# Scores' products with the keys' low parts: 64 rows each, in pairs in the two halves of the array, and attention in pieces of 256 queries

## The chip, the cores and the metric

The kernel runs on one core of one Trainium2 chip. The metric is the device time of one execution in microseconds (us), as a median of several runs. The kernel before takes 960.17 us (three runs, 958.83 to 961.95).

The core has a matrix engine (TensorE, PE in the profile; its weight loads are listed as PEld), VectorE (DVE), ScalarE (ACT), GpSimd (POOL) and SyncE (SP), which issues nearly all DMAs. Matrix products land in PSUM, which has eight buffers of 128 partitions by 512 floats (banks).

## The reference

One layer of an encoder block over 512 positions of width 2048, in float32: adaptive RMSNorm, one projection, two token mixers side by side, a gated output projection and a final RMSNorm. The change touches the first mixer, attention with 16 heads of 64:

```python
aq, ak, av, ag, gq, gk, gv, gg, lr_f, lr_b = jnp.split(h @ w_in[layer], PROJ_SPLITS, axis=-1)
for window, dilation in ((128, 1), (512, 4), (2048, 16)):
    o_p, lse_p = dilated_window_attention(aq, ak, av, rel_bias, window, dilation)
    ...
mix_w = jax.nn.softmax(jnp.stack(lses, axis=0), axis=0)
att = jnp.einsum('pbsh,pbshe->bshe', mix_w, jnp.stack(outs, axis=0))
```

Inside, logits are `q.k / 8` plus a bias by distance, with a mask. Three window softmaxes merged by their denominators are one softmax over all 512 keys, in which a key counts as often as it lies in a window: the kernel computes that, with the logarithm of this multiplicity in the bias.

## The kernel before

**Precision.** TensorE multiplies a rounded float32 format (`F32R`, fp32r in the profile). To keep float32 accuracy the kernel splits operands into a rounded high part and the rest, the low part, and sums the products high x high, low x high and high x low (`three`, lines 168 to 171: three matmuls, each with its own weight load). A matmul has a stationary operand (the weights, up to 128 rows by 128 columns) and a moving one (the same rows by up to 512 columns).

**Stages.** First a starting stage computes the normalised input and a first part of the projection (`sta`, `stb` in the profile). Then the projection goes on in units of 512 columns (`unit`, line 843): `qk2`, `qk4`, `qk6` (queries and keys of two pairs of heads each), `gk`, then `gv0` and so on for the second mixer, and the output projection. A unit has four tiles of 128 columns (in PSUM buffers with the tag `pj`, five of them) and eight groups of weights, each fetched on SP one or two groups ahead, and split into high and low part by ScalarE (L313) and VectorE (L297). One call of `three` is a tick; a unit has 64.

**Side work.** Into a unit's stream of matmuls, work of other kinds is hung at given shares of its ticks. TensorE's order is the order of the program. Side items are emitted with a raised priority; the order on the other engines is set by a scheduler from priorities and dependences, ahead of time, so that on the chip each engine works off a fixed queue. A side item due at share `at` is emitted after the first tick that is at least 64 x `at`; an item due at 1 or later goes over into the next unit. The sums for the gates (`rawv`, `rawg`) are other side work, on VectorE.

**Attention** (`attention`, line 556) is side work of the units `qk2`, `qk4`, `qk6` and `gk`, four heads in each call. It works in tiles of 128 queries: 16 tiles in a call, and for each

- `score` (line 567): two matmuls (L576, L577) into a PSUM buffer with the tag `pa`, of which there are three; VectorE adds the bias and finds the row minimum (L580), ScalarE takes the exponential (L583), VectorE the reciprocal (L584), GpSimd scales (L585). The result is `p`.
- `turn` (line 589), two tiles later: four transposes (L597) of `p` into a `pa` buffer, which ScalarE (L601) and VectorE (L602) evict as high and low part, `pt`.
- `values` (line 605), once for two tiles, a half: eight matmuls (L611) of `pt` with the values, into a `pa` buffer, evicted by ScalarE (L614) and VectorE (L618).

The items of a call are spread evenly over 0.8 of the unit's ticks from 0.17 on (`ATT_AT`), the first two moved forward by 0.04 and 0.05, the last moved back by 0.05, into the next unit.

**Operands of the scores.** `qk_evict` (line 531) runs after the unit that made a pair of heads. Each head has 64 rows in the banks `psq` and `psk`. For a head, `qs` has 128 rows: the high part of the queries (ScalarE, L539) in the head's own half of the rows, the low part (VectorE, L540) in the other half. `ks` has the keys' high part in both halves, `kl` the keys' low part in both: own half by an engine (L548, L550), the other by a DMA. So

```python
mm(ps, qs[:, q], ks, start=True, stop=False)   # high x high + low x high
mm(ps, qs[:, q], kl, start=False, stop=True)   # high x low  + low x low
```

The banks of the first two pairs come from the starting stage: its eight tiles use the five `pj` buffers and the three `pa` buffers, in which stand the keys of the first pair and queries and keys of the second.

Of the kernel before, what the change touches and what calls it, by code (L numbers as in the profile page):

```python
# [10 lines left out]
F32 = mybir.dt.float32  # L11
F32R = mybir.dt.float32r
I32 = mybir.dt.int32
AF = mybir.ActivationFunctionType
ALU = mybir.AluOpType
# [3 lines left out]
P = 128  # L19
# [114 lines left out]
def block_kernel(ctx: ExitStack, tc: tile.TileContext, a: dict):  # L134
    nc = tc.nc
# [6 lines left out]
    sm = ctx.enter_context(tc.tile_pool(name="sm", bufs=4))  # L142
# [4 lines left out]
    def T2(name, dt=F32, parts=P):  # L147
        return t2.tile([parts, 512], dt, tag="t2", name=name)

    def B8(name, shape, dt=F32):  # L150
        return b8.tile([P] + shape, dt, tag="b8", name=name)
# [4 lines left out]
    def PA(name):  # L156
        return pp.tile([P, 512], F32, tag="pa", bufs=3, name=name)

    mm = nc.tensor.matmul
    tt = nc.vector.tensor_tensor  # L160
    stt = nc.vector.scalar_tensor_tensor
    act = nc.scalar.activation
# [69 lines left out]
    for j in range(4):  # L232
        ch, cl = c_parts[2 * j][64:65, :], c_parts[2 * j + 1][64:65, :]
        src = first[64:65, 512 * j:512 * j + 512]
# [92 lines left out]
    scale = cst.tile([P, KT], F32, tag="scale", name="scale")  # L327
# [149 lines left out]
    n = len(chain) // 2  # L477
    for z in range(2):
        task(("row", z), "DVE", 0.66, [("ul", 0)], 950, lambda z=z: bias_row_out(z), None, "b8" if z else None)
    for i in range(n):  # L480
        mm_task(i)
        st, k, j = chain[i]
# [15 lines left out]
    for i in range(n, 2 * n):  # L498
        mm_task(i)
        st, k, j = chain[i]  # L500
# [3 lines left out]
    for w in range(4):  # L504
        for kt in range(4):
            j, g = w // 2 * 4 + kt, w % 2
# [22 lines left out]
    stacks = {}  # L529

    def qk_evict(p, psq, psk):

        for j in range(2):
            own = slice(64 * j, 64 * j + 64)
            oth = slice(64 - 64 * j, 128 - 64 * j)
            qs = T2(f"qs{p}{j}", F32R)
            act(qs[own], psq[own, ::-1], AF.Copy, scale=-0.125)  # L539
            stt(qs[oth], psq[own, ::-1], -0.125, qs[own].bitcast(F32),  # L540
                op0=ALU.mult, op1=ALU.subtract)
            stacks[2 * p + j] = [qs, None, None, own]
        for j in range(2):
            own = slice(64 * j, 64 * j + 64)
            oth = slice(64 - 64 * j, 128 - 64 * j)
            ks = T2(f"ks{p}{j}", F32R)
            kl = T2(f"kl{p}{j}", F32R)
            act(ks[own], psk[own], AF.Copy)  # L548
            nc.sync.dma_start(ks[oth].bitcast(F32), ks[own].bitcast(F32))
            tt(kl[own], psk[own], ks[own].bitcast(F32), op=ALU.subtract)  # L550
            nc.sync.dma_start(kl[oth].bitcast(F32), kl[own].bitcast(F32))
            stacks[2 * p + j][1:3] = ks, kl
# [2 lines left out]

    def attention(pairs):

        tiles = [(2 * p + j, i) for p in pairs for j in range(2) for i in range(4)]
        gt, pt, pr_ = {}, {}, {}
        heads = [2 * p + j for p in pairs for j in range(2)]  # L560

        def g_load(h):
            g = gp.tile([P, 896], F32, tag="g", name=f"g{h}")
            nc.sync.dma_start(g, bass.AP(grow.tensor, grow.offset + h * 1024, [[1, P], [1, 896]]))
            gt[h] = g

        def score(h, i):
            def go():
                if h % 8 == 0 and i == 0:
                    cat[h // 8] = B8(f"cat{h // 8}", [4, 512])  # L570
                if i == 1 and h != heads[-1]:
                    g_load(h + 1)
                qs, ks, kl, _ = stacks[h]
                q = slice(P * i, P * i + P)
                ps = PA(f"s{h}{i}")
                mm(ps, qs[:, q], ks, start=True, stop=False)  # L576
                mm(ps, qs[:, q], kl, start=False, stop=True)  # L577
                t = T2(f"p{h}{i}")
                st = sm.tile([P, 3], F32, tag="st", name=f"st{h}{i}", bufs=6)
                nc.vector.tensor_tensor_reduce(  # L580
                    out=t, in0=ps, in1=gt[h][:, P * i:P * i + 512], op0=ALU.add, op1=ALU.min,
                    scale=1.0, scalar=3e38, accum_out=st[:, 0:1])
                act(t, t, AF.Exp, bias=st[:, 0:1], scale=-1.0, accum_out=st[:, 1:2])  # L583
                nc.vector.reciprocal(st[:, 2:3], st[:, 1:2])  # L584
                nc.gpsimd.tensor_scalar(t, t, st[:, 2:3], 1.0, op0=ALU.mult, op1=ALU.mult)  # L585
                pr_[h, i] = t
            return go

        def turn(h, i):
            def go():  # L590
                half, ii = divmod(i, 2)
                if ii == 0:
                    pt[h, half] = B8(f"pt{h}{half}", [2, 4, 256], F32R)
                t = pr_.pop((h, i))
                pk = PA(f"t{h}{i}")
                for kt in range(4):
                    nc.tensor.transpose(pk[:, kt * P:kt * P + P], t[:, kt * P:kt * P + P], ident)  # L597
                hi = pt[h, half][:, 0, :, P * ii:P * ii + P]
                lo = pt[h, half][:, 1, :, P * ii:P * ii + P]
                src = pk.rearrange("p (k q) -> p k q", k=4)  # L600
                act(hi, src, AF.Copy)  # L601
                tt(lo, src, hi.bitcast(F32), op=ALU.subtract)  # L602
            return go

        def values(h, half):
            def go():
                t = pt.pop((h, half))
                po = PA(f"o{h}{half}")
                for kt in range(4):
                    for w in range(2):  # L610
                        mm(po[:, :256], vv[h // 4][:, kt, h % 4, :], t[:, w, kt, :],  # L611
                           start=kt == 0 and w == 0, stop=kt == 3 and w == 1)
                oh = sm.tile([64, 256], F32, tag="oh", name=f"oh{h}{half}", bufs=1)
                act(oh, po[64:128, :256], AF.Copy)  # L614
                own = stacks[h][3]
                p = h // 2
                dst = cat[p // 4][own, p % 4, 256 - 256 * half:512 - 256 * half]
                tt(dst[:, ::-1], po[0:64, :256], oh, op=ALU.add)  # L618
            return go

        items = []
        n = len(tiles)
        for x in range(n + 4):
            if x < n:
                items.append(score(*tiles[x]))
            if 2 <= x <= n + 1:
                items.append(turn(*tiles[x - 2]))
            if 3 <= x <= n + 2 and tiles[x - 3][1] % 2 == 1:
                items.append(values(tiles[x - 3][0], tiles[x - 3][1] // 2))
        g_load(heads[0])  # L630
        start, span, move0, move1, move_last = ATT_AT
        at = [start + (q + 0.5) / len(items) * span for q in range(len(items))]
        at[0] -= move0
        at[1] -= move1
        at[-1] += move_last
        return list(zip(at, items))
# [52 lines left out]
    def some_sums(name):  # L689
        r = [sum_work.pop(0) for _ in range(SUMS_IN.get(name, len(sum_work)))]  # L690
        n = len(r)
        loads = [(max(q - 0.3, 0.1) / n, x[0]) for q, x in enumerate(r)]
        return sorted(loads + [((q + 0.7) / n, x[1]) for q, x in enumerate(r)], key=lambda x: x[0])
# [206 lines left out]
    for p in range(2):  # L900
        qk_evict(p, psb["b", 4 + 2 * p], psb["b", 5 + 2 * p])
    for n, p in (("qk2", 0), ("qk4", 2), ("qk6", 4)):
        ps = unit(n, False, attention((p, p + 1)) + ([(0.05, shift_row)] + some_sums(n) if p == 4 else []))
        for q in range(2):
            qk_evict(p + 2 + q, ps[2 * q], ps[2 * q + 1])

    ps = unit("gk", False, attention((6, 7)) + some_sums("gk"))
    gla["k"] = B8("gkt", [4, 512])
    for i in range(4):
# [17 lines left out]
    ps = unit("gv0", True, some_sums("gv0"), lr=lr_tick)  # L927
# [20 lines left out]
    ps = unit("gv1", True, gla_head(0) + some_sums("gv1"))  # L948
# [3 lines left out]
    for j in range(2):  # L952
        ps = unit(f"ag{j}", False, gla_head(1 + j) + some_sums(f"ag{j}"))
        gate_evict(ps, cat[j], f"a{j}", vbias[:, 4 * j:4 * j + 4])
    ps = unit("gg0", False, gla_head(3) + some_sums("gg0"))
# [16 lines left out]
    ps = unit("gg1", False, side + some_sums("gg1"))  # L972
# [43 lines left out]
    for j in range(3):  # L1016
# [3 lines left out]
        ps = unit(f"o{j}", True, side, rhs=rhs)  # L1020
# [22 lines left out]
    for tiles in ((0, 1), (2,), (3,)):  # L1043
        ps = unit("o3", True, rhs=rhs, tiles=tiles)
# [86 lines left out]
```

## Time and profile before

| | |
|---|---|
| median of three runs | 960.17 us (958.83 to 961.95) |
| the profiled execution | 959.9 us, of which the instructions span 957.9 us |
| TensorE busy / weight loads | 98% / 81% of the span |
| VectorE, ScalarE, GpSimd busy | 63%, 45%, 8% |
| granted TensorE clock, mean | 0.997 |
| attention's matmuls | from 198.0 to 459.1 us |
| of these: scores | 64 with `ks`, 64 with `kl`, each 128 rows by 512 columns |

Times inside an execution are counted from the span's start. A row of a timeline has start, duration, engine, line, operation, the tiles (out <- in, buffer numbers left out), sizes and count; in brackets stands the idle time of the engine before it, and what ended it. Matmuls are pipelined: a record's duration is longer than the distance to the next, and its end is modelled.

### The profile page before, as it was taken

Reading aid. Unit: us, or ns where it says so; the run is one execution under the profiler, and the core shown is the slowest. Engines: PE = TensorE matmul, PEld = TensorE weight load, DVE = VectorE, ACT = ScalarE, POOL = GpSimd, SP = SyncE. Lnnn points to the kernel's source line nnn. Section 1 sums busy time; section 2 is a strip of 40 time slices with the busy share of each in tenths; the row PEclk is TensorE's granted clock in tenths of the full one; section 3 lists DMA queues with packets and bytes.
Section 4 is the critical chain, followed back from the end, with each engine's and each line's share of the span. In section 5 each row is a group of like instructions: output and inputs, shape, how many; then the busy total and the mean of one; then the engine's idle time right before and its main releaser. Section 6 shows DMA issues by size and latency. Waiting matters only on the chain.

```text
span 957.9 us, 11999 instructions
## 1 busy us (share of the span) xinstructions
PE 939.7 (98%) x4464; PEld 777.1 (81%) x4464; DVE 605.3 (63%) x900; ACT 431.5 (45%) x719; POOL 81.1 (8%) x100
## 2 busy tenths in 40 slices
PE   8999999999999999999999999999999999999996
PEld 5888788888888888888778888888887888888884
DVE  7988899675756676766435656675964352546421
ACT  5443533565655655655215544543834152233222
POOL 0000000012122022122000000000010000202120
PEclk9999999999999999999999999999999999999998
DMA  9999687443333463533454244354555464244013
GB/s 330 413 411 365 229 296 275 150 131 105 112 103 105 144 200 108 173 127 103 150 176 146 86 132 154 132 176 154 173 195 183 132 221 154 92 151 152 23 55 121
DMA packets 45180, 163.76 MB, mean 171 GB/s; under 512 B 5730, under 2 KB 6018, under 8 KB 40386
## 3 DMA queue, kind: packets, MB, share of 16 engines
q1 hardware_dynamic: 44946, 162.68, 49.9%
q8 instruction: 35, 0.57, 0.2%
q10 hardware_dynamic: 176, 0.33, 0.1%
q14 instruction: 23, 0.18, 0.1%
HBM read 154.51 MB, written 4.28 MB: 166 GB/s over the span
## 4 chain that ended last, share of the span: by engine, by line
PE 84%; DMA 6%; DVE 5%; issue 3%; ACT 1%; SPq 0%; POOL 0%; ACTq 0%; DVEq 0%; POOLq 0%
PE ps_o L170 6%; PE ps_o L169 6%; PE ps_o L171 6%; DMA rawg<-in_wg 6%; PE ps_qk L170 5%; PE ps_qk L169 5%; PE ps_qk L171 5%; PE o L611 3%; PE sta L169 3%; PE sta L170 3%; PE sta L171 3%; PE stb L171 3%; PE stb L169 3%; PE stb L170 3%; PE ps_gv L171 3%; PE ps_gv L170 3%
## 5 line engine op out<-in xcount | busy, mean ns | idle before, releaser
L585 POOL TENSOR_SCALAR p<-p,st 128x512 f32<-128x512 f32 x64 | 45.5, 711 | 406.6 <-DVE st L584 357.9
L244 DVE CUSTOM_DVE_ANT_0 cb<-cb,sb,c_bcond 128x2048 f32<-128x2048 f32 (+1 forms) x32 | 73.4, 2294 | 0.0
L583 ACT ACTIVATE p<-p,st 128x512 f32<-128x512 f32 x64 | 46.1, 721 | 56.8 <-DVE st L580 56.3
L602 DVE TENSOR_TENSOR pt<-t,pt 128x512 fp32r<-128x512 f32 x64 | 44.0, 689 | 16.2 <-ACT pt L601 15.8
L580 DVE CUSTOM_DVE_ANT_0 p<-s,g 128x512 f32<-128x512 f32 x64 | 43.6, 687 | 14.8 <-PE s L577 14.5
L601 ACT ACTIVATE pt<-t 128x512 fp32r<-128x512 f32 x64 | 37.8, 592 | 10.2 <-PE t L597 9.2
L244 DVE CUSTOM_DVE_ANT_0 rawg<-rawg,sb,gate 128x1024 f32<-128x1024 f32 x16 | 20.5, 1283 | 29.6 <-DMA rawg<-in_wg 29.6
L611 PEld LDWEIGHTS o<-pt,vv 128*128 128x128 f32 x256 | 34.7, 188 | 5.0 <-DVE pt L602 2.2
L597 PEld LDWEIGHTS t<-c_ident,p 128*128 128x128 f32 x256 | 31.8, 140 | 8.5
L597 PE MATMUL t<-c_ident,p 128*128 128x128 f32 x256 | 38.3, 272 | 0.0
L611 PE MATMUL o<-pt,vv 128*128 128x256 f32 x256 | 36.6, 283 | 0.9 <-DVE pt L602 0.8
L244 DVE CUSTOM_DVE_ANT_0 rawg<-rawg,sb,c_bcond 128x1024 f32<-128x1024 f32 x16 | 20.5, 1283 | 26.3 <-DMA rawg<-in_wg 26.3
L1014 POOL TENSOR_TENSOR x<-x,fgain 128x512 f32<-128x512 f32 x12 | 20.3, 1696 | 185.3 <-ACT ysq L1012 185.3
L1012 ACT ACTIVATE ysq<-x 128x512 f32<-128x512 f32 x16 | 10.1, 632 | 47.2 <-DVE x L1010 47.2
L767 POOL TENSOR_SCALAR dc<-st,sc 128x256 f32<-128x256 f32 x16 | 10.4, 652 | 245.5 <-DVE st L764 240.6
L1009 DVE TENSOR_TENSOR y<-ps_o,sb 128x512 f32<-128x512 f32 x16 | 10.9, 684 | 25.9 <-PE ps_o L171 25.9
L584 DVE RECIPROCAL st<-st 128x1 f32<-128x1 f32 x64 | 10.3, 162 | 24.9 <-ACT p L583 24.9
L576 PE MATMUL s<-ks,qs 128*128 128x512 f32 x64 | 25.1, 391 | 0.0
L577 PE MATMUL s<-kl,qs 128*128 128x512 f32 x64 | 25.0, 391 | 0.0
L774 ACT ACTIVATE sq<-st,sc 128x256 f32<-128x256 f32 x24 | 12.2, 509 | 26.8 <-DVE st L769 14.3
L1010 DVE TENSOR_TENSOR x<-y,x 128x512 f32<-128x512 f32 x16 | 18.0, 1125 | 0.3
L614 ACT ACTIVATE oh<-o 64x256 f32<-64x256 f32 x32 | 12.2, 382 | 13.0 <-PE o L611 12.2
(1275 smaller groups left out, 2916.7 us busy)
## 6 DMA issues: line engine op xcount, KB each, us to landing
cb<-in_wm SPq DMA_DIRECT2D x31, 1024.0 KB, 7.9
rawg<-in_wg SPq DMA_DIRECT2D x32, 512.0 KB, 3.4
raw_o<-in_w_o SPq DMA_DIRECT2D x32, 512.0 KB, 3.4
raw_qk<-in_w_qk SPq DMA_DIRECT2D x24, 512.0 KB, 3.4
rawb<-in_w_sb SPq DMA_DIRECT2D x16, 512.0 KB, 4.8
rawv<-in_wv SPq DMA_DIRECT2D x16, 512.0 KB, 3.8
raw_gv<-in_w_gv SPq DMA_DIRECT2D x16, 512.0 KB, 3.5
raw_ag<-in_w_ag SPq DMA_DIRECT2D x16, 512.0 KB, 3.3
```

What stands on the lines that cost most here:

```text
L169: mm(ps, lh, rh, start=first, stop=False)
L170: mm(ps, ll, rh, start=False, stop=False)
L171: mm(ps, lh, rl, start=False, stop=last)
L244: nc.vector.tensor_tensor_reduce(out=w, in0=w, in1=with_, op0=ALU.mult, op1=ALU.add, scale=1.0, scalar=init, accum_out=dst)
L576: mm(ps, qs[:, q], ks, start=True, stop=False)
L580: nc.vector.tensor_tensor_reduce(out=t, in0=ps, in1=gt[h][:, P * i:P * i + 512], op0=ALU.add, op1=ALU.min, scale=1.0, scalar=3e38, accum_o ...
L583: act(t, t, AF.Exp, bias=st[:, 0:1], scale=-1.0, accum_out=st[:, 1:2])
L585: nc.gpsimd.tensor_scalar(t, t, st[:, 2:3], 1.0, op0=ALU.mult, op1=ALU.mult)
L597: nc.tensor.transpose(pk[:, kt * P:kt * P + P], t[:, kt * P:kt * P + P], ident)
L601: act(hi, src, AF.Copy)
L602: tt(lo, src, hi.bitcast(F32), op=ALU.subtract)
L611: mm(po[:, :256], vv[h // 4][:, kt, h % 4, :], t[:, w, kt, :], start=kt == 0 and w == 0, stop=kt == 3 and w == 1)
```

## The change

- `qk_evict`: in the blocks 0 and 2 of 128 queries the high part stays in the head's own rows and the low part in the others; in the blocks 1 and 3 the two change places. Each of the two instructions per head becomes two, over 2 x 128 columns each.
- `score` takes a half (two blocks, 256 queries) and two `pa` buffers. Both products with `ks` come first, over 128 rows as before. The product with `kl` takes only the rows with the queries' high part: own rows for the first block, the other rows for the second. The two stand in different halves of the array's rows. Low x low is left out.
- The items are now, per half: score of half x, values of half x - 2, the two transposes of half x - 1. A call has 32 items instead of 40, spread over the same share of the unit. The load of the next head's bias stands in the head's first score.

```diff
--- before.py
+++ after.py
@@ -532,14 +532,17 @@
 
 
 
+
         for j in range(2):
             own = slice(64 * j, 64 * j + 64)
             oth = slice(64 - 64 * j, 128 - 64 * j)
             qs = T2(f"qs{p}{j}", F32R)
-            act(qs[own], psq[own, ::-1], AF.Copy, scale=-0.125)
-            stt(qs[oth], psq[own, ::-1], -0.125, qs[own].bitcast(F32),
-                op0=ALU.mult, op1=ALU.subtract)
-            stacks[2 * p + j] = [qs, None, None, own]
+            for z, (rows, others) in enumerate(((own, oth), (oth, own))):
+                src = psq[own, ::-1].rearrange("p (a z c) -> p a z c", z=2, c=P)[:, :, z, :]
+                hi, lo = (qs[r].rearrange("p (a z c) -> p a z c", z=2, c=P)[:, :, z, :] for r in (rows, others))
+                act(hi, src, AF.Copy, scale=-0.125)
+                stt(lo, src, -0.125, hi.bitcast(F32), op0=ALU.mult, op1=ALU.subtract)
+            stacks[2 * p + j] = [qs, None, None, own, oth]
         for j in range(2):
             own = slice(64 * j, 64 * j + 64)
             oth = slice(64 - 64 * j, 128 - 64 * j)
@@ -555,7 +558,6 @@
 
     def attention(pairs):
 
-        tiles = [(2 * p + j, i) for p in pairs for j in range(2) for i in range(4)]
         gt, pt, pr_ = {}, {}, {}
         heads = [2 * p + j for p in pairs for j in range(2)]
 
@@ -564,26 +566,31 @@
             nc.sync.dma_start(g, bass.AP(grow.tensor, grow.offset + h * 1024, [[1, P], [1, 896]]))
             gt[h] = g
 
-        def score(h, i):
+        def score(h, half):
+
             def go():
-                if h % 8 == 0 and i == 0:
+                if h % 8 == 0 and half == 0:
                     cat[h // 8] = B8(f"cat{h // 8}", [4, 512])
-                if i == 1 and h != heads[-1]:
+                if half == 0 and h != heads[-1]:
                     g_load(h + 1)
-                qs, ks, kl, _ = stacks[h]
-                q = slice(P * i, P * i + P)
-                ps = PA(f"s{h}{i}")
-                mm(ps, qs[:, q], ks, start=True, stop=False)
-                mm(ps, qs[:, q], kl, start=False, stop=True)
-                t = T2(f"p{h}{i}")
-                st = sm.tile([P, 3], F32, tag="st", name=f"st{h}{i}", bufs=6)
-                nc.vector.tensor_tensor_reduce(
-                    out=t, in0=ps, in1=gt[h][:, P * i:P * i + 512], op0=ALU.add, op1=ALU.min,
-                    scale=1.0, scalar=3e38, accum_out=st[:, 0:1])
-                act(t, t, AF.Exp, bias=st[:, 0:1], scale=-1.0, accum_out=st[:, 1:2])
-                nc.vector.reciprocal(st[:, 2:3], st[:, 1:2])
-                nc.gpsimd.tensor_scalar(t, t, st[:, 2:3], 1.0, op0=ALU.mult, op1=ALU.mult)
-                pr_[h, i] = t
+                qs, ks, kl, own, oth = stacks[h]
+                q = [slice(P * i, P * i + P) for i in (2 * half, 2 * half + 1)]
+                ps = [PA(f"s{h}{half}{z}") for z in range(2)]
+                for z in range(2):
+                    mm(ps[z], qs[:, q[z]], ks, start=True, stop=False)
+                for z, rows in enumerate((own, oth)):
+                    mm(ps[z], qs[rows, q[z]], kl[rows], start=False, stop=True)
+                for z in range(2):
+                    i = 2 * half + z
+                    t = T2(f"p{h}{i}")
+                    st = sm.tile([P, 3], F32, tag="st", name=f"st{h}{i}", bufs=6)
+                    nc.vector.tensor_tensor_reduce(
+                        out=t, in0=ps[z], in1=gt[h][:, P * i:P * i + 512], op0=ALU.add, op1=ALU.min,
+                        scale=1.0, scalar=3e38, accum_out=st[:, 0:1])
+                    act(t, t, AF.Exp, bias=st[:, 0:1], scale=-1.0, accum_out=st[:, 1:2])
+                    nc.vector.reciprocal(st[:, 2:3], st[:, 1:2])
+                    nc.gpsimd.tensor_scalar(t, t, st[:, 2:3], 1.0, op0=ALU.mult, op1=ALU.mult)
+                    pr_[h, i] = t
             return go
 
         def turn(h, i):
@@ -619,14 +626,16 @@
             return go
 
         items = []
-        n = len(tiles)
-        for x in range(n + 4):
+        halves = [(h, half) for h in heads for half in range(2)]
+        n = len(halves)
+        for x in range(n + 2):
             if x < n:
-                items.append(score(*tiles[x]))
-            if 2 <= x <= n + 1:
-                items.append(turn(*tiles[x - 2]))
-            if 3 <= x <= n + 2 and tiles[x - 3][1] % 2 == 1:
-                items.append(values(tiles[x - 3][0], tiles[x - 3][1] // 2))
+                items.append(score(*halves[x]))
+            if 2 <= x:
+                items.append(values(*halves[x - 2]))
+            if 1 <= x <= n:
+                h, half = halves[x - 1]
+                items += [turn(h, 2 * half), turn(h, 2 * half + 1)]
         g_load(heads[0])
         start, span, move0, move1, move_last = ATT_AT
         at = [start + (q + 0.5) / len(items) * span for q in range(len(items))]
```

## The prediction

> **What bounds the kernel now.** I read the page's busy shares and its chain first, then the windows over attention, then TensorE's own order of instructions.
>
> ```profile
> span 957.9 us, 11999 instructions
> PE 939.7 (98%) x4464; PEld 777.1 (81%) x4464; DVE 605.3 (63%) x900; ACT 431.5 (45%) x719; POOL 81.1 (8%) x100
> ...
> PE 84%; DMA 6%; DVE 5%; issue 3%; ACT 1%; SPq 0%; POOL 0%; ACTq 0%; DVEq 0%; POOLq 0%
> ...
> L611 PE MATMUL o<-pt,vv 128*128 128x256 f32 x256 | 36.6, 283 | 0.9 <-DVE pt L602 0.8
> ...
> L614 ACT ACTIVATE oh<-o 64x256 f32<-64x256 f32 x32 | 12.2, 382 | 13.0 <-PE o L611 12.2
> ```
>
> TensorE is busy 98% of the span and carries most of the chain. The windows (PE, PEld, DVE, ACT, POOL busy, then the granted clock) say the same of the stretch that the change touches:
>
> ```profile
> 220.00:260.00 40.00, 39.97 (x220) 33.76 (x219) 26.36 (x55) 24.47 (x47) 6.28 (x9) 1.00 0.32 101
> 330.00:400.00 70.00, 69.97 (x369) 58.83 (x369) 50.06 (x104) 38.41 (x74) 11.13 (x16) 1.00 0.53 166
> 400.00:455.00 55.00, 54.16 (x295) 45.59 (x294) 36.48 (x82) 30.91 (x62) 12.05 (x16) 1.00 0.37 119
> ```
>
> VectorE has a third of its time free, ScalarE nearly half, and the clock is full. The only visible wait of TensorE in attention is the 0.8 us for `pt` in the `o` row. So time taken from TensorE's stream here comes off the end, and any new wait of TensorE is added to it. What a matmul of 512 columns really costs is not its recorded 0.39 us but the distance to the next; the timeline has 32 of them from 329.84 to 336.86:
>
> ```profile
> 329.84 0.39 PE L170 MATMUL ps_qk<-h_hi,qk60l 128*128 128x512 f32 x1
> ...
> 336.86 0.40 PE L171 MATMUL ps_qk<-h_lo,qk61h 128*128 128x512 f32 x1
> ```
>
> (336.86 - 329.84) / 31 = 0.2265 us, for the scores' products as for the projection's. The other 0.16 us of a record (0.39 - 0.23) is its tail, in which the next already runs.
>
> **Removed: half of the passes with the low keys.** There are 64 such passes (16 heads x 4 blocks). After the change they are 32 pairs; the two of a pair stand in different rows of the array and write different PSUM buffers. If they run at once, one pass of 0.2265 us goes per pair: 32 x 0.2265 = 7.25 us. Three things can reduce that.
>
> First, **the weights**. A load now begins where the previous matmul begins, as these starts show (matmuls, then loads):
>
> ```profile
> 300.64 0.39 PE L576 MATMUL s<-ks,qs 128*128 128x512 f32 x1
> 300.87 0.39 PE L577 MATMUL s<-kl,qs 128*128 128x512 f32 x1
> ```
>
> ```profile
> 300.42 0.19 PEld L576 LDWEIGHTS s<-ks,qs 128*128 128x128 f32 x1
> 300.65 0.19 PEld L577 LDWEIGHTS s<-kl,qs 128*128 128x128 f32 x1
> 300.87 0.19 PEld L169 LDWEIGHTS ps_qk<-h_hi,qk45h 128*128 128x128 f32 x1
> ...
> 302.11 0.19 PEld L169 LDWEIGHTS ps_qk<-h_hi,qk45h 128*128 128x128 f32 x1
> 302.22 0.19 PEld L170 LDWEIGHTS ps_qk<-h_hi,qk45l 128*128 128x128 f32 x1
> ```
>
> Behind a short transpose the next load follows after 0.11 us. Two loads of 0.11 us fit under the one 0.2265 us pass ahead of the pair, provided that the second half's load need not wait until the first half's matmul has begun. If it must, the second matmul starts 0.11 us late. Bounds 0 and 0.11 us a pair; I take 0, because the two halves hold separate weights, and keep the other end as a rival. By the Trainium skill (TensorE: Matmul & The Clock Gate, "Part 3: Packing small matmuls — row/col tiling") loads to other row groups overlap and tiles start about 4 ns apart, which would take 0.1 us off the gain; no run here shows it.
>
> Second, **the change of the array's shape**. The trace has one neighbour, the low-rank gate's products, which use 64 of 128 columns between full matmuls:
>
> ```profile
> 464.81 0.39 PE L171 MATMUL ps_gv<-gv00l,h_hi 128*128 128x512 f32 x1
> 465.04 0.40 PE L924 MATMUL plr<-h_hi,lrs 128*64 128x512 f32 x1
> 465.27 0.39 PE L925 MATMUL plr<-h_lo,lrs 128*64 128x512 f32 x1
> 465.50 0.39 PE L169 MATMUL ps_gv<-gv01h,h_hi 128*128 128x512 f32 x1
> ```
>
> Going in and coming out the distance stays 0.23 us: at most 0.01 us per visit. But that is half the columns, not half the rows. Bounds for a pair: 0.01 us (this row) and twice the tail, 2 x 0.16 = 0.32 us, if the array runs empty before and after; I take 0.01, the nearer row. The Trainium skill (TensorEngine Tiling (Array Packing), "Key Properties") says that changing the tiling mode, not merely the tile, drains TensorE. By that rule the gain would turn into a loss, which is a rival below; the `plr` rows do not show such a drain.
>
> Third, the halves might not run at once at all: gain 0, a rival too. As taken, 32 x (0.2265 - 0.01) = **6.9 us saved**.
>
> **Added: finer evictions of the queries.** Per head, one ScalarE and one VectorE instruction over 512 columns become two of each over 256.
>
> ```profile
> L539 ACT ACTIVATE qs<-ps_qk x12: 582/593/595, 251.6 to 392.2; 64x512 fp32r<-64x512 f32 x12
> L540 DVE SCALAR_TENSOR_TENSOR qs<-ps_qk,qs x12: 684/688/694, 252.4 to 393.4; 64x512 fp32r<-64x512 f32 x12
> ```
>
> ```profile
> 254.58 0.42 DVE L618 TENSOR_TENSOR cat<-o,oh 64x256 f32<-64x256 f32 x1
> ```
>
> With the 64x256 rows (ScalarE 0.38 in the `oh` row above, VectorE 0.42) a query bank, which both engines read by turns, takes 4 x (0.38 + 0.42) = 3.2 us instead of 2 x (0.59 + 0.69) = 2.56 us: 0.64 us, with two more handovers 0.7. Engine time (16 x 0.17 on ScalarE, 16 x 0.15 on VectorE) is covered by their free share; only the later release of a bank can reach TensorE. Bounds for that: 0, and the first stall below.
>
> **Moved: attention in halves.** A score item now takes two of the three attention PSUM buffers at once. In the steady state (28 of 32 halves) the order is score, values, turn, turn; the second tile of a score reuses the buffer of a transpose two items back, and values follow the last transpose of their half after 3 or 4 ticks of projection less its own work. These rows of the chain show the distance now (transposes of a half at 206.56 and, of the next tile, 209.54; values of the first half at 210.68):
>
> ```profile
> 206.56 0.44 PE t L597 x4
> ...
> 209.54 0.44 PE t L597 x4
> 210.68 0.94 PE o L611 x8
> ```
>
> From 207.00 to 210.68 are 3.7 us. After: 3 ticks of 0.68 us (3 x 0.2265) and a score of three slots (0.68) make 2.7 us; the eviction that must fit in is 0.59 (ScalarE) + 0.69 (VectorE) = 1.3 us plus what stands ahead in the two queues. Taken at nothing, covered by this 1.4 us; if a weight split (1.23 us below) and a sum of the other work meet there, a half waits some tenths: bound 0.25 us x 28 = 7 us. The p tiles get more time, not less (five items between score and transpose instead of four). SP's load of the next head's bias moves one score earlier; it waits for the previous head's last reduction, and the weight fetches behind it on SP run one to two groups (8 ticks, 5.4 us each) ahead: nothing.
>
> **The start of each attention call** is where I charge a stall. The first two scores stand one tick apart (now at ticks 9 and 10 of 64, then at 10 and 11), and together want four buffers where there are three. The second's second tile needs the first's first tile to be reduced. VectorE, first in the first call, then in the second, and TensorE there:
>
> ```profile
> 196.89 0.69 DVE L540 SCALAR_TENSOR_TENSOR qs<-stb,qs 64x512 fp32r<-64x512 f32 x1 [0.66 <-ACT qs L539]
> ...
> 199.91 0.69 DVE L550 TENSOR_TENSOR kl<-stb,ks 64x512 fp32r<-64x512 f32 x1
> 200.63 0.69 DVE L580 CUSTOM_DVE_ANT_0 p<-s,g 128x512 f32<-128x512 f32 x1
> ```
>
> ```profile
> 265.00 1.23 DVE L297 TENSOR_TENSOR qk43l<-raw_qk,qk43h 128x1024 fp32r<-128x1024 f32 x1 [2.40 <-ACT qk43h L313]
> 266.26 0.69 DVE L580 CUSTOM_DVE_ANT_0 p<-s,g 128x512 f32<-128x512 f32 x1
> ```
>
> ```profile
> 197.99 0.39 PE L576 MATMUL s<-ks,qs 128*128 128x512 f32 x1
> ...
> 264.39 0.39 PE L576 MATMUL s<-ks,qs 128*128 128x512 f32 x1
> ```
>
> Calls 2 to 4: the first score starts a tick later, 264.39 + 0.68 = 265.07; the second 0.68 + 0.68 later, its second tile 0.23 after that: 266.66. The reduction ahead cannot start before 266.26 (a weight split stands before it) and ends 266.95: 0.3 us each, 0.9 in all. Call 1: the attention buffers still hold three banks of the starting stage. First score 198.67, second 200.03; its first tile takes the bank of the second pair's keys, released at 199.91 + 0.69 = 200.60 now and 0.7 to 1.4 us later with one or two longer query banks ahead: a wait of 1.3 to 2.0 us. The reduction behind it ends another 0.7 us on, where the second tile would have come after 0.23: 0.5 more. I take 2.2 us. Together **3.1 us lost**, bounds 0.5 (the order on VectorE turns out kinder) and 7.
>
> **Sum.** 959.9 us of the profiled execution - 6.9 + 3.1 = 956.1. It ran 0.3 us under the median of 960.17, so against that median: **956.4 us**, 0.4% faster. Its own range: 953.8 (stalls of 0.5) to 960.
>
> **The rivals.**
> - *The second half's weights wait.* For: every load in the trace begins at a matmul's begin. Against: no two loads there go to separate rows. Gain 32 x (0.2265 - 0.11 - 0.01) = 3.4; 959.9 - 3.4 + 3.1 + 0.3 = 959.9: no change.
> - *The array takes the halves in turn*, so the change doesn't do what it says. For: no two matmuls in the trace start closer than their columns take. Against: none of them use different rows. 959.9 + 3.1 + 0.3 = 963.3.
> - *The array runs empty at each pair* (the other side): slower. Place: the two seams of each pair; price 0.16 us each, the tail of the matmul rows. 32 x (0.32 - 0.2265) = 3.0 lost instead of 6.9 saved: 959.9 + 3.0 + 3.1 + 0.3 = 966.3. It decides from (7.25 - 3.1) / 64 = 0.065 us per seam on. Against it the `plr` rows. This is the drain of the skill's rule; its chance is that of row halves behaving otherwise than column halves.
> - *The order waits*: `pt` comes late in the steady state, 0.25 us x 28 = 7 us, and eats the gain: 956.4 + 7 = 963.4. For: 2.7 us instead of 3.7, and a VectorE busy 0.66 of 220 to 260 and 0.72 of 330 to 400. Against: 1.3 us of work in it.
>
> **How the numbers follow.** A measurement of this kernel tells about 0.3% (2.9 us) from no change: faster is under 957.3, slower over 963.1. Forecast 0.50 (0.36 faster, 0.13 same, 0.01 slower); weights wait 0.16 (0.02, 0.13, 0.01); halves in turn 0.10 (0, 0.04, 0.06); array runs empty 0.10 (all slower); order waits 0.14 (0, 0.06, 0.08). Sums: 0.38 faster, 0.36 same, 0.26 slower. The range, 953.8 to 966.3, reaches from the forecast's best stalls to the middle of the slow case.
>
> **What would show it.** Pair right: in the timeline the two `s<-kl,qs` matmuls, 64 rows each, start within 0.02 us, and the next matmul 0.23 us later. Weights wait: starts 0.11 us apart. In turn: 0.23 apart. Running empty: the first of them 0.39 behind its forerunner instead of 0.23. Stalls: gaps in TensorE's starts near 200 (some 2 us) and near 266, 332 and 398 (0.3 us), put down to `p` or `kl`; the order rival: waits of `o` for `pt` above 3 us in all. The forecast is wrong if attention's stretch shortens by less than 2.9 us.

## The result, and the profile after

The changed kernel takes 971.17 us (median of six runs, 967.21 to 972.53) against 958.87 us before (six runs): a ratio of 1.0123, 95% interval 1.0108 to 1.0137. It is 12 us slower; 956.4 was forecast, and the range (up to 966.3) did not reach it.

The page of the changed kernel, cut to the span, the busy shares and the scores' products with `ks` (count; busy, mean ns; idle time before them and what ended it):

```profile
span 970.4 us, 12023 instructions
PE 949.8 (98%) x4464; PEld 770.1 (79%) x4464; DVE 611.0 (63%) x916; ACT 435.0 (45%) x735; POOL 83.3 (9%) x100
...
L580 PE MATMUL s<-ks,qs 128*128 128x512 f32 x64 | 21.0, 407 | 2.2 <-DVE qs L544 2.2
```

TensorE is as busy as before, 98%, but over a span that is 12.5 us longer: its idle time grows by only 2.4 us, so most of the loss hides inside "busy". In the stretch of attention the profile names three waits of TensorE that the kernel before did not have:

```profile
PE s L580 <- DVE qs L544: 2.2, 1, 2.2
PE ps_gk L169 <- DVE qs L544: 1.2, 1, 1.2
...
PE ps_qk L169 <- DVE qs L544: 0.2, 1, 0.2
```

All three are for the new, finer eviction of the queries. The windows (same columns as before; the clock is the third number from the end):

```profile
200.00:220.00 20.00, 18.00 (x76) 13.14 (x77) 10.67 (x26) 8.99 (x21) 4.11 (x6) 0.83 0.35 103
220.00:260.00 40.00, 40.00 (x214) 31.75 (x213) 24.00 (x53) 21.53 (x42) 6.91 (x10) 1.00 0.28 88
...
330.00:400.00 70.00, 69.99 (x364) 55.21 (x363) 49.95 (x106) 40.30 (x81) 12.91 (x16) 1.00 0.50 159
```

From 220 to 260 us TensorE does not wait at all (40.00 of 40.00). Of these windows only the first, in the first attention call, shows time lost openly, and there the clock is not full. The timeline of TensorE there:

```profile
199.38 0.39 PE L580 MATMUL s<-ks,qs 128*128 128x512 f32 x1
202.00 0.76 PE L580 MATMUL s<-ks,qs 128*128 128x512 f32 x1 [2.23 <-DVE qs L544]
202.69 0.79 PE L582 MATMUL s<-kl,qs 64*128 64x512 f32 x2
203.42 0.79 PE L169 MATMUL ps_qk<-h_hi,qk21h 128*128 128x512 f32 x1
204.01 0.63 PE L170 MATMUL ps_qk<-h_hi,qk21l 128*128 128x512 f32 x1
204.44 0.63 PE L171 MATMUL ps_qk<-h_lo,qk21h 128*128 128x512 f32 x1
```

```profile
202.00:208.50 6.50, 6.50 (x15) 3.86 (x16) 3.60 (x12) 2.61 (x7) 1.03 (x2) 0.50 0.41 121
```

The second `ks` product, still of the first score, starts 2.62 us after the one at 199.38, 2.4 us more than the usual 0.23. Behind it matmuls stand 0.43 us apart instead of 0.23: for 6.5 us the granted clock is 0.50, worth 3.2 us. This profiled execution, of 972.53 us, is the slowest of the six, so its low clock may be more than is usual.

And the pairs themselves, in a place where nothing waits (matmuls, then weight loads):

```profile
214.03 0.62 PE L580 MATMUL s<-ks,qs 128*128 128x512 f32 x2
214.59 0.50 PE L582 MATMUL s<-kl,qs 64*128 64x512 f32 x2
215.02 0.50 PE L169 MATMUL ps_qk<-h_hi,qk22h 128*128 128x512 f32 x1
215.36 0.40 PE L170 MATMUL ps_qk<-h_hi,qk22l 128*128 128x512 f32 x1
```

```profile
213.81 0.42 PEld L580 LDWEIGHTS s<-ks,qs 128*128 128x128 f32 x2
214.59 0.19 PEld L582 LDWEIGHTS s<-kl,qs 64*128 64x128 f32 x2 [0.36 <-issue]
215.02 0.19 PEld L169 LDWEIGHTS ps_qk<-h_hi,qk22h 128*128 128x128 f32 x1 [0.24 <-issue]
215.12 0.19 PEld L170 LDWEIGHTS ps_qk<-h_hi,qk22l 128*128 128x128 f32 x1
```

The two matmuls of a pair do run at once: one row of 0.50 us holds both, and the next matmul starts 0.43 us after them. But from the first `ks` product at 214.03 to L170 at 215.36 are 1.33 us, where five passes of the kernel before, which do the same work, took 5 x 0.2265 = 1.13. The pair's weights are not loaded under the `ks` product: the load begins at 214.59, with the matmul itself. The same happens on the way back, at 215.02. A pair loses about 0.2 us instead of gaining 0.2.

### The profile page after: what moved, and what is told of

Its sections match the earlier page's. It is cut to its first block, busy times and chain, and to the rows that moved or that the text cites. A ratio compares the mean times of both kernels' runs of the same rounds, so it can differ in the third digit from the quotient of the medians.

```text
span 970.4 us, 12023 instructions
## 1 busy us (share of the span) xinstructions
PE 949.8 (98%) x4464; PEld 770.1 (79%) x4464; DVE 611.0 (63%) x916; ACT 435.0 (45%) x735; POOL 83.3 (9%) x100
## 4 chain that ended last, share of the span: by engine, by line
PE 87%; DVE 4%; ACT 3%; DMA 3%; issue 2%; SPq 0%; POOL 0%; ACTq 0%; DVEq 0%; POOLq 0%
PE ps_o L171 6%; PE ps_o L170 6%; PE ps_o L169 6%; PE ps_qk L169 5%; PE ps_qk L170 4%; PE ps_qk L171 4%; PE sta L169 3%; PE sta L170 3%; PE sta L171 3%; PE stb L171 3%; PE ps_gv L171 3%; PE ps_gv L170 3%; PE ps_gv L169 3%; PE stb L170 3%; PE stb L169 3%; PE o L618 3%
## 5 line engine op out<-in xcount | busy, mean ns | idle before, releaser
L592 POOL TENSOR_SCALAR p<-p,st 128x512 f32<-128x512 f32 x64 | 47.9, 755 | 414.2 <-DVE st L591 396.3
L609 DVE TENSOR_TENSOR pt<-t,pt 128x512 fp32r<-128x512 f32 x64 | 43.9, 688 | 25.8 <-ACT pt L608 25.6
L580 PE MATMUL s<-ks,qs 128*128 128x512 f32 x64 | 21.0, 407 | 2.2 <-DVE qs L544 2.2
L689 DVE CUSTOM_DVE_ANT_0 rawv<-rawv,shb 128x1024 f32<-128x1024 f32 x8 | 10.7, 1331 | 12.7 <-DMA rawv<-in_wv 12.7
L580 PEld LDWEIGHTS s<-ks,qs 128*128 128x128 f32 x64 | 12.4, 194 | 6.2 <-issue 2.6
```

The lines of the kernel that those rows point to most:

```text
L580: mm(ps[z], qs[:, q[z]], ks, start=True, stop=False)
```

## The experiments

My theory after this reading was that each visit to 64 rows (a stretch of 64-row matmuls between full ones) costs two seams, one in and one out, and that the finer eviction, not the order in halves, makes the waits. Its rivals were the order (a score that takes two buffers), and that only two matmuls at once, not the change of shape, cost time. Each run below has the ratio to the kernel before, measured beside it, with its 95% interval.

### Full rows in the changed kernel

```diff
-                for z, rows in enumerate((own, oth)):
-                    mm(ps[z], qs[rows, q[z]], kl[rows], start=False, stop=True)
+                for z in range(2):
+                    mm(ps[z], qs[:, q[z]], kl, start=False, stop=True)
```

> The changed kernel with the low keys' products over all 128 rows again (low x low is back in), the order in halves and the finer eviction kept. Seams theory (a visit to 64 rows costs two seams of 0.2 us, so a pair takes 0.63 us where two full passes took 0.45): 32 x 0.177 = 5.7 us less than the changed kernel, about 965.5 us, and 6 to 7 us over before remain, from the first call's wait and its low clock and from the waits for projection banks. Order theory (nearly all of the loss is the order in halves): within 2 us of the changed kernel, 969 to 973. If the pairs were worth their predicted 6.9 us: 978.

Measured: 964.07 us, ratio 1.0068 (1.0042 to 1.0094). Against the changed kernel's 1.0123 that is 0.55% or 5.3 us less, near the 5.7 us of the seams; from the two intervals this difference is uncertain by some 3 us. So the pairs are a loss, and another 6.5 us come with the order or the eviction. The wait of 2.2 us in the first call is still there, but in this profiled execution only some 3.5 us at half clock follow it, not 6.5.

### The finer eviction alone, in the kernel before

```diff
-            act(qs[own], psq[own, ::-1], AF.Copy, scale=-0.125)
-            stt(qs[oth], psq[own, ::-1], -0.125, qs[own].bitcast(F32), op0=ALU.mult, op1=ALU.subtract)
+            for z, (rows, others) in enumerate(((own, oth), (oth, own))):
+                ...  # as in the change: one act and one stt over 2 x 128 columns each
```

> The kernel before with the finer eviction of the queries alone: order and products as before, and complete. Eviction theory (the waits of the changed kernel at the starts of the calls, 2.4 us at 199, 0.3 at 270, 0.2 at 338 and 1.4 at 406, come from banks that are released later, and the idle 2.4 us makes the clock fall for some 6 us, worth 3 us): 4 to 8 us over before, 963 to 967. Order theory (the waits come from a score that takes two buffers at once): within 2 us of before, 957 to 961.

Measured: 965.04 us, ratio 1.0072 (1.0055 to 1.0089): 7 us, with no other part of the change. TensorE's waits in this kernel are those of the changed one, in the same places, and the clock of the first call falls as well:

```profile
PE s L578 <- DVE qs L543: 2.0, 1, 2.0
PE ps_gk L169 <- DVE qs L543: 1.2, 1, 1.2
...
PE ps_qk L169 <- DVE qs L543: 0.2, 1, 0.2
```

```profile
200.00:220.00 20.00, 18.20 (x85) 15.04 (x86) 11.96 (x27) 10.32 (x21) 3.49 (x5) 0.91 0.37 103
```

### 64 rows, not paired, in the kernel before

```diff
-                mm(ps, qs[:, q], kl, start=False, stop=True)
+                mm(ps, qs[own, q], kl[own], start=False, stop=True)
```

> The kernel before with the low keys' product over the head's own 64 rows, not paired (low x low left out): 64 single visits to 64 rows, nothing else changed. Seams theory: each visit costs 0.40 us more than a full pass, 64 x 0.40 = 26 us, about 985 us. Rival (going to 64 rows is free, as with 64 columns; only two matmuls at once disturb each other): 958 to 960, no change.

Measured: 982.87 us, ratio 1.0257 (1.0240 to 1.0274), 25 us more. Nothing stands beside the 64-row matmul here, so the cost is the change of shape. TensorE's matmuls and loads at one visit:

```profile
215.42 0.39 PE L576 MATMUL s<-ks,qs 128*128 128x512 f32 x1
215.74 0.49 PE L577 MATMUL s<-kl,qs 64*128 64x512 f32 x1
216.16 0.50 PE L169 MATMUL ps_qk<-h_hi,qk23h 128*128 128x512 f32 x1
216.50 0.40 PE L170 MATMUL ps_qk<-h_hi,qk23l 128*128 128x512 f32 x1
```

```profile
215.74 0.18 PEld L577 LDWEIGHTS s<-kl,qs 64*128 64x128 f32 x1 [0.35 <-issue]
216.16 0.19 PEld L169 LDWEIGHTS ps_qk<-h_hi,qk23h 128*128 128x128 f32 x1 [0.24 <-issue]
216.27 0.19 PEld L170 LDWEIGHTS ps_qk<-h_hi,qk23l 128*128 128x128 f32 x1
```

From 215.42 to 216.50 are 1.08 us for three passes, against 3 x 0.2265 = 0.68: 0.40 us a visit, x 64 = 25.6. These starts suggest how it divides, if a load that nothing covers takes 0.11 us (the distance 216.16 to 216.27) and the rest is the array running out. From the `ks` product to the next load: 0.32 = 0.2265 + 0.09, the array running out. From that load to the next: 0.42 = 0.11 for the load, which nothing covers, + 0.2265 + 0.09 of running out again. Then 0.11 for the full weights, again uncovered. By this division a seam is 0.09 + 0.11 = 0.20 us; the 0.40 us of a visit are measured, the two parts are an estimate.

The drain that the Trainium skill states (TensorEngine Tiling (Array Packing), "Key Properties": a change of tiling mode drains TensorE) agrees with the 0.40 us of a visit to half the rows; its page gives no price. By the division above, more than half of the 0.20 us is the weight load that follows in the open.

### 96 rows

```diff
-                mm(ps, qs[:, q], kl, start=False, stop=True)
+                r = slice(0, 96) if h % 2 == 0 else slice(0, P)
+                mm(ps, qs[r, q], kl[r], start=False, stop=True)
```

> The kernel before with the low keys' product over 96 rows instead of 128 for every second head (32 passes; half of low x low is left out there). Theory that the seams belong to the array's shape (64 rows are run as one of two halves, 96 rows in the undivided array): no change, 957 to 959, and full passes behind it at 0.23 us. Rival (any change of the number of rows makes the array run empty): 32 x 0.40 = 12.8 us more, 971.

Measured: 958.40 us, ratio 0.9999 (0.9989 to 1.0008). There is no seam: 96 rows cost nothing, 64 rows do. So the price does not come with every number of rows under 128. A `ks` product, the 96-row product and the two full passes behind it start at 300.76, 300.99, 301.22 and 301.46. The matmuls of that tile keep their durations:

```profile
L578 PE MATMUL s<-kl,qs x64: 387/393/403, 198.1 to 448.8; 96*128 96x512 f32 x32, 128*128 128x512 f32 x32
```

### Each pair twice

```diff
-                for z, rows in enumerate((own, oth)):
-                    mm(ps[z], qs[rows, q[z]], kl[rows], start=False, stop=True)
+                for n in range(2):
+                    for z, rows in enumerate((own, oth)):
+                        mm(ps[z], qs[rows, q[z]], kl[rows], start=False, stop=n == 1)
```

> The changed kernel with each pair issued twice in one visit (high x low is added twice). It gives the price of a further pair inside a visit. If the halves' weights load under the running pair: 0.23 us each, 32 x 0.23 = 7.3 us over the changed kernel, 978. If each pair also pays its loads in the open (0.11 us): 10.7 us, 982. If every pair runs empty like a visit of its own: 20 us, 991.

Measured: 978.60 us, ratio 1.0208 (1.0193 to 1.0223), 0.85% or 8 us over the changed kernel, uncertain by some 2 us; expected were 7.3. In the timeline the four matmuls take the place of two:

```profile
213.17 0.73 PE L583 MATMUL s<-kl,qs 64*128 64x512 f32 x4
213.83 0.50 PE L169 MATMUL ps_qk<-h_hi,qk22h 128*128 128x512 f32 x1
```

From their start to the next are 0.66 us, where one pair took 215.02 - 214.59 = 0.43: a further pair costs 0.23 us, one pass, with its loads covered. So a visit costs 0.40 us once and 0.23 us per pair. As full passes the pair's two products take 0.45 us, so n pairs save n x 0.23 - 0.40: -0.17 us for one, +0.06 for two. Two pairs would need four score banks at once, and the pool has three; 16 such visits would save about 1 us, an estimate from these rows that no kernel was run for.

### Without the low keys' products

```diff
                 mm(ps, qs[:, q], ks, start=True, stop=False)
-                mm(ps, qs[:, q], kl, start=False, stop=True)
```

(with `stop=True` in the line that stays)

> The kernel before without the products with the keys' low parts (64 full passes left out, so high x low and low x low are missing). If time taken from TensorE's stream in attention comes off the end, as the prediction assumed: 64 x 0.2265 = 14.5 us less than before, about 943.5 us. Rival (another engine or the transfers take over as the bound): less than 10 us.

Measured: 946.01 us, ratio 0.9867 (0.9850 to 0.9883): 12.4 of the 14.5 us come off the end (11.2 to 14.4 by the interval). The assumption holds in the main. The missing 2 us are not all located; a part is a new wait in the now denser stream:

```profile
PE s L576 <- DVE st L579: 1.1, 1, 1.1
```

### The first attention call later

```diff
         start, span, move0, move1, move_last = ATT_AT
+        if pairs[0] == 0:
+            start, span = start + 0.07, span - 0.07
```

> The changed kernel with the first attention call begun later (from 0.24 of the unit's ticks instead of 0.17, spread over 0.73 instead of 0.80). The first score then comes about 2.7 us later, when the banks of the starting stage are free. Theory: the 2.4 us wait at 199 goes, and with it the stretch of half clock behind it (some 15 matmuls at 0.43 us instead of 0.23, 3 us): about 5 us less than the changed kernel, 966. Rival (the clock falls for another reason): 2.4 us less, 968.8. Rival (the denser items wait elsewhere): no change.

Measured: 968.36 us, ratio 1.0106 (1.0087 to 1.0124), 0.17% or 1.6 us less than the changed kernel, and the intervals overlap: inconclusive as to the time. The trace shows what took the gain. The wait at 199 and its low clock are gone (clock 1.00 from 185 to 220), but the denser items wait near the call's end, at 253 and 254 us, and behind that the matmuls stand 0.43 us apart from 255.4 to 258. The gate's weights (`plr`, in the unit after attention) come later too: TensorE waits 2.1 us for them, 0.9 in the changed kernel. The first two waits, and the window around them:

```profile
PE o L618 <- DVE pt L609: 1.0, 1, 1.0
...
PE o L618 <- ACT pt L608: 0.5, 1, 0.5
```

```profile
220.00:260.00 40.00, 38.51 (x205) 30.62 (x204) 21.85 (x51) 21.23 (x44) 6.88 (x10) 0.96 0.28 88
```

### The finer eviction for the first two pairs alone

```diff
+            if p < 2:
+                ...  # the finer eviction
+            else:
                 ...  # the one before
```

> The kernel before with the finer eviction for the first two pairs of heads alone, those of the starting stage. Theory (the wait of 2.2 us for the query bank in front of the first scores, and some 3 us more because the clock is halved behind it): 5 us over before, 963; the other 2 us of the finer eviction belong to the three later calls. Rival (the clock is no part of it): 2.2 us over before, 960.

Measured: 961.99 us, ratio 1.0044 (1.0029 to 1.0060), 4 us, between the two expectations: more than the wait of 2.0 us alone. Its ten runs spread from 959.7 to 966.7, those of before beside it from 956.9 to 961.4. In the profiled execution half clock follows the wait for some 3 us, worth 1.6 us; with the wait that makes 3.6. So the clock behind the wait is part of the cost. But this execution is also the slowest of the ten (966.73 us): it has a wait of 2.9 us at 730, far from attention (`gn`, 1.2 us in the kernel before), with another 3 us of half clock behind it. Not all of the spread belongs to the eviction.

### The order in halves alone

The changed kernel with full rows (the first diff above) and, besides, the eviction of before (the second diff taken back), so that the order of the items is all that is left of the change.

> The changed kernel's order in halves alone: the old eviction of the queries, and the low keys' products over all 128 rows, not paired. If the order costs nothing in itself, as the prediction's first term for it said: no change against before, or up to 0.9 us less, since the one wait of TensorE for the transposed weights at the end of attention (0.8 us) should go: 957 to 959. The predicted stalls of the first two scores (0.3 us in three calls, 2.2 us in the first) would give 3 us more, 961. Order rival (late transposed weights in the steady state): 7 us more.

Measured: 960.47 us, ratio 1.0023 (1.0010 to 1.0035), 2 us: between the two expectations. The two-buffer score does wait in the first call, but little (0.3 for `kl`, 0.2 for `st`), and once more in the fourth (0.3 for `pt`); the wait for `pt` at the end of attention is gone. The largest new wait is outside attention, where the low-rank gate's weights now come late (0.4 us in the kernel before):

```profile
PE plr L931 <- DVE lrs L924: 1.6, 1, 1.6
...
PE s L578 <- DVE kl L551: 0.3, 1, 0.3
PE s L578 <- DVE pt L607: 0.3, 1, 0.3
PE s L578 <- DVE st L585: 0.2, 1, 0.2
```

### The eviction regrouped

Why should 0.6 us more work per bank make TensorE wait for 2 us? VectorE in the changed kernel, at the bank of the second pair's queries:

```profile
196.88 0.42 DVE L544 SCALAR_TENSOR_TENSOR qs<-stb,qs 64x256 fp32r<-64x256 f32 x1
197.74 0.42 DVE L544 SCALAR_TENSOR_TENSOR qs<-stb,qs 64x256 fp32r<-64x256 f32 x1 [0.44 <-ACT qs L543]
198.61 0.43 DVE L544 SCALAR_TENSOR_TENSOR qs<-stb,qs 64x256 fp32r<-64x256 f32 x1 [0.45 <-ACT qs L543]
199.22 0.68 DVE L553 TENSOR_TENSOR kl<-stb,ks 64x512 fp32r<-64x512 f32 x1 [0.19 <-ACT ks L551]
200.17 1.23 DVE L297 TENSOR_TENSOR qk23l<-raw_qk,qk23h 128x1024 fp32r<-128x1024 f32 x1 [0.26 <-ACT qk23h L313]
201.43 0.43 DVE L544 SCALAR_TENSOR_TENSOR qs<-stb,qs 64x256 fp32r<-64x256 f32 x1
```

Each of the four VectorE instructions needs the result of a ScalarE instruction on the same bank, and each next one of ScalarE comes after VectorE is done. Between the third and the fourth stand another eviction and a weight split (on ScalarE as well, up to 200.13): the bank is released at 201.86, where the kernel before had it at 197.58. If the handovers are the cause, emitting a bank's four ScalarE instructions first should remove it:

```diff
                 act(hi, src, AF.Copy, scale=-0.125)
-                stt(lo, src, -0.125, hi.bitcast(F32), op0=ALU.mult, op1=ALU.subtract)
+                todo.append((lo, src, hi))
             stacks[2 * p + j] = [qs, None, None, own]
+        for lo, src, hi in todo:
+            stt(lo, src, -0.125, hi.bitcast(F32), op0=ALU.mult, op1=ALU.subtract)
```

> The kernel before with the finer eviction of the queries alone, but with the four ScalarE instructions of a bank emitted ahead of the four of VectorE, so that the bank changes hands once and not seven times. Theory (the finer eviction costs 7 us because each handover waits for the other engine's fixed queue, in which weight splits of 1.0 and 1.2 us stand; the instructions' own 0.6 us more are harmless): at most 2 us over before, 957 to 960. Rival (the longer work itself, or the 64x256 shape with a step, is what holds the banks): 5 to 7 us over before, 963 to 965.

Measured: 960.37 us, ratio 1.0022 (1.0012 to 1.0032): 2 us instead of 7. The instructions are the same in number and size, so not their length but their taking turns was the cost. In the first call TensorE is busy 20.00 of 20 us at full clock. What is left is waits elsewhere, above all one in the third call:

```profile
PE t L602 <- DVE st L585: 1.7, 1, 1.7
```

```profile
200.00:220.00 20.00, 20.00 (x107) 16.84 (x106) 12.65 (x32) 11.15 (x23) 4.88 (x7) 1.00 0.41 123
```

In the whole change:

> The changed kernel with the same regrouped eviction. Theory: the waits at the call starts and the half clock behind the first go, the seams of the 32 pairs (5.7 us) and up to 2 us of the order stay: 6 to 8 us over before, 964 to 966, some 5 us less than the changed kernel. Rival (waits return with two buffers per score): 969 to 971. That the pairs pay once the waits are gone: under 958.

Measured: 967.21 us, ratio 1.0095 (1.0079 to 1.0110), 0.28% or 2.7 us less than the changed kernel, where some 5 were expected; the two intervals just touch. The first wait and its clock are gone, but three waits for projection banks remain (1.1 us in two places at the starts of the middle calls, 0.6 in the last), and 1.6 us for the gate's weights:

```profile
PE plr L936 <- DVE lrs L929: 1.6, 1, 1.6
...
PE ps_qk L169 <- DVE qs L548: 1.1, 2, 0.6
PE ps_gk L169 <- DVE qs L548: 0.6, 1, 0.6
```

With the best eviction found, the change is still 9 us slower than before: some 5.7 by the price of the seams, and the waits above, 3.3 together (of which 0.4 for the gate's weights was there before). No version with pairs beat the kernel before, and by the arithmetic of the visits, an estimate from these rows, none with one pair per visit can.

## Why the prediction was wrong

**That TensorE's stream is the bound** was right in the main: leaving out 64 passes of 0.2265 us brought 12.4 of 14.5 us.

**The pair** was right as a picture (both matmuls in one row of the timeline) and wrong as a price. The step that failed first is the second of the three reductions, the change of the array's shape: "I take 0.01, the nearer row". The `plr` row was near only in looks. It halves the columns; the pair halves the rows, and that costs 0.40 us a visit, 40 times the value taken. The sum's term of 6.9 us saved is 5.3 to 5.7 us lost, an error of more than 12 us. With every other term as predicted, it alone turns 3.8 us faster into some 8.6 slower. The rest of the miss, 3.4 us, lies in the evictions and the order: 3.1 us charged, 6.5 measured with full rows.

**Its upper bound** was too low as well: 0.32 us, twice the tail of 0.16. By the division above a seam has 0.09 of running out, less than the tail, but also 0.11 of a weight load that is no longer covered. I had the load's 0.11 us in the paragraph before and did not add it at the seam. With it the running-empty rival would have read 2 x (0.16 + 0.11) = 0.54 us, and the range would have reached past the measured time. That rival, given a chance of 0.10, is what happened, at a higher price and with more lost elsewhere; its threshold of 0.065 us per seam was passed three times over.

**The weights** (0 taken): inside a visit they are covered, as taken; each pair issued twice shows it. At the seams they are not.

**The finer evictions** were the second failure. I priced the instructions (0.7 us a bank, right) and let only the first call's start pay. Measured alone they cost 7 us: the handovers between two engines with fixed queues let weight splits in between, the bank that the first call needs came 4 us later, and behind the wait in the first call the clock was halved, for some 3 us with this eviction alone and for 6.5 in the changed kernel's profile. The clock's part (1.6 and 3.2 us) was in no step.

**The starts of the calls**: 2.2 us were charged to the first call and 2.4 were measured, but that they agree is luck. The charge was for the second score, which takes the bank of the keys and then waits for a reduction; with the order alone that is 0.5 us. The wait measured is in the first score, for the queries' bank. The 0.3 us in each of three later calls did not come; there TensorE waits for projection banks instead, and its matmuls start 0.2 to 1.4 us late.

**The order in halves** was taken at nothing in the steady state, and there it is next to nothing (40.00 of 40.00 us busy; 0.3 us once in the fourth call). Alone it costs 2 us; its profile shows 1.2 us more of waiting at the unit after attention, a place that no step named, and what the rest is stays open. The order rival (7 us of late `pt`) did not happen.

The three parts do not add up (5.3 + 6.9 + 2.2 against 12): order and eviction wait in the same place of the first call, and the order removes the one wait of before. How the rest divides between them is not settled.

## What to carry to other kernels

Before pairing small matmuls in halves of the array, count visits, not matmuls: in a stream of full matmuls a visit to 64-row halves costs 0.40 us here, as much as nearly two passes of 512 columns, so by this estimate it takes at least two pairs per visit to gain. A neighbour in the trace gives a bound only if it changes the same thing; and the upper bound of a drain has to include the weight load that can no longer run ahead. When an eviction is split between two engines that share a bank, count the handovers, since at each one the other engine's queue can let something else in; grouping by engine brought back 5 of 7 us with the same instructions.

## What the runs showed of the hardware that was not expected

- Going from full matmuls to 64 rows and back cost 0.40 us a visit; half the columns (`plr`, 64 of 128) and 96 rows don't show such a price, with matmuls 0.23 to 0.24 us apart throughout.
- The two matmuls of a pair lie in one row of 0.50 us, where one alone took 0.49. This agrees with the Trainium skill (TensorE: Matmul & The Clock Gate, "Part 3: Packing small matmuls — row/col tiling"), by which tiles start some nanoseconds apart; that page's loads that overlap by row group hold inside a visit only.
- Behind some waits of TensorE the granted clock stood at 0.50, and the length of the wait alone does not decide it. A wait of 2.2 us was followed by 6.5 us of half clock in the changed kernel, but by 3 to 3.5 us with full rows and with each pair twice; waits of 2.0 us (the finer eviction alone) by some 3 us; the two of 0.5 and 1.0 us close together (the first call later) by some 3 us. A wait of 1.2 us at 407 in the changed kernel, one of 1.7 with the regrouped eviction, and two of 2.1 for the gate's weights (the first call later, and each pair twice) were not followed by it. What decides is not settled here.
